# Global attention scores: q's low part against k's high part alone, in two 64-row halves of TensorE

## The chip, the cores and the metric

The kernel runs on one NeuronCore of a Trainium2 chip. The metric is the device time of one execution in microseconds (us). The profile comes from one execution on the chip, recorded by the hardware profiler; its times count from the first instruction.

## What is computed

One layer of a diffusion backbone over 1024 latent tokens of width 1024, with 256 context tokens. The input is modulated by a conditioning vector and projected. Two attention branches work on the projections: a windowed one (branch 0, the key blocks next to a block of 128 queries, a sink logit for each head) and a global one (branch 1, all keys, with root-mean-square norm of q and k). Both add the context's keys to the same softmax. Each branch has 8 query heads of width 64 and 2 key heads. Their outputs are gated, merged and projected; a feed-forward part with a short convolution follows. Cut to what the change touches:

```python
def _gqa_scores(q, k):
    return jnp.einsum("bqhgd,bkhd->bhgqk", q, k).astype(jnp.float32) * (HEAD_DIM ** -0.5)

def _global_attention(q, k_all, v_all):
    ...
        p = jax.nn.softmax(_gqa_scores(q_blk, k_all), axis=-1)
        return _gqa_values(p, v_all)
```

## The kernel before

Most products are formed from split numbers: a float32 value is stored as a high part, rounded to the format that TensorE reads in one pass (R32), and a low part, the rest (`split`, line 80). `mm3` (line 89) then needs three matmuls: high by high, high by low, low by high.

The projections come first. The windowed q, the k and v of both branches and the gates are computed group by group; PSUM tiles are emptied by a queue of small steps (`side_step`, line 681). `kv_post` (line 343) handles one tile of 128 tokens of k and v: step `s1` stores v and starts norm and rotary, `s2` ends them and splits the four key heads (two of each branch) into `ks` (line 370), a tile of 128 tokens by 4 heads by 128 columns: 64 columns of k's high part, then 64 of its low part. `s3` transposes each head on TensorE (line 376), so that the high part comes to lie in partitions 0 to 63 and the low part in 64 to 127, and ScalarE copies the result into `KL[h]` (line 379; 128 partitions by 1024 tokens). Context keys go to `KC` (line 381).

Attention is cut into 32 units (`class Unit`): 16 of the windowed branch, then 16 of the global one. A unit is one block of 128 queries and one key head, with its 4 query heads. `qprep` (line 397) runs two units ahead: GpSimd splits q into `qs`, high part and low part next to each other; four transposes (line 404) bring it into a PSUM tile `tr` (high in partitions 0 to 63, low in 64 to 127; inside attention this tile comes from the pool `pt` of three, which the transposes of the probabilities use too). ScalarE copies it into `q1` (line 407), and two DMAs of SP's queue (lines 408 and 409) write the halves of `q1` into the other halves of `q2`. So `q1` holds high over low, and `q2` low over high.

`qk` (line 412) makes one score tile with two matmuls over all 128 rows: `q1` against k gives high by high plus low by low, `q2` against k gives low by high plus high by low. The sum is the product with all four terms. `lat` (line 425) does a head: in the global branch it calls `qk` for each half of 512 of the 1024 latent keys (lines 441 and 442), each half into its own PSUM bank of the tile `s`. VectorE then scales and takes the maximum (line 459), ScalarE exponentiates (line 426). `cxp` (line 464) does the context's keys for the four heads of a global unit. `value_steps` transposes the probabilities (`ptr`, line 531), splits them (`pth`, `ptl`, lines 540 and 541, some on GpSimd) and multiplies with v (`av`, lines 552 and 553); `rows` (line 496) transposes the sums of the softmax (`str`, line 498).

The steps of a unit's scores, of the values of the unit before and, from the third global unit on, of the windowed branch's output product (`branch_steps`, tiles `b`, lines 90 to 92 by `mm3`) are interleaved in the main loop (line 833). A scheduler of the language's tile layer orders the instructions of each engine from there, within the dependencies, before the program is built; each engine then runs its own list in order.

Of the kernel before, what the change touches and what calls it, by code (L numbers as in the profile page):

```python
# [7 lines left out]
F32 = mybir.dt.float32  # L8
# [5 lines left out]
P = 128  # L14
D = 1024
T = 1024
NC = 256
KT = 8
NT = 8
HD = 64  # L20
# [7 lines left out]
HALF = 512  # L28
# [41 lines left out]
def layer_kernel(  # L70
# [6 lines left out]
    nc = tc.nc  # L77
# [152 lines left out]
    for k in range(KT):  # L230
# [5 lines left out]
        for t in range(NT):  # L236
            s = slice(t * P, (t + 1) * P)
# [96 lines left out]
    KL, KC, VT = [], [], []  # L334
# [8 lines left out]
    def kv_post(t, kv):  # L343
        st = {}
        kb = kv[:, 128:256].rearrange("p (h d) -> p h d", d=HD)

        def s1():
            vt = VT[t // 2][:, t % 2]
            v3 = kv[:, 256:512].rearrange("p (h d) -> p h d", d=HD)
            nc.scalar.copy(vt[:, :, 0:HD], v3)  # L350
            tp = pw(f"ktp{t}")
            st["tp"] = tp = [tp[:, n * P:(n + 1) * P] for n in range(4)]
            st["ss"] = rms_scale(kb, 2, f"k{t}", tp[3])
            if t < NT:
                st["tb"] = ph1.tile([P, 2, HD], F32, tag="tb", name=f"tbk{t}", bufs=4)
                gfold(st["tb"], 1, t, nc.vector)
                rope(nc.vector, kv[:, 0:128], kv[:, 0:128], 2, ropec[:, t], ropes[:, t], f"ka{t}", tp[0], tp[1])
            nc.gpsimd.tensor_tensor(out=vt[:, :, HD:P], in0=v3, in1=vt[:, :, 0:HD].bitcast(F32), op=ALU.subtract)

        def s2():  # L360
            rms_apply(kb, 2, st["ss"])
            tp = st["tp"]
            if t < NT:
                tb = st["tb"]
                rope(nc.vector, kv[:, 128:256], kv[:, 128:256], 2, tb[:, 0], tb[:, 1], f"kb{t}", tp[2], tp[3])
            else:
                nc.gpsimd.tensor_tensor(out=kb, in0=kb, in1=bc(gcol[:, 1], 2), op=ALU.mult)
            st["ks"] = ks = pw(f"ks{t}", (P, 4, P), R32)
            k3 = kv[:, 0:256].rearrange("p (h d) -> p h d", d=HD)
            split(k3, ks[:, :, 0:HD], ks[:, :, HD:P], nc.vector, nc.vector)  # L370

        def s3():
            ks = st["ks"]
            tr = acc_tile(f"ktr{t}", R32).rearrange("p (h q) -> p h q", h=4)
            for h in range(4):
                nc.tensor.transpose(tr[:, h], ks[:, h], identr)
            if t < NT:
                for h in range(4):
                    nc.scalar.copy(KL[h][:, t * P:(t + 1) * P], tr[:, h])
            else:  # L380
                nc.scalar.copy(KC[0][:, :, (t - NT) * P:(t - NT + 1) * P], tr)
        return [s1] + [lambda: None] * GAP + [s2, s3]

    class Unit:
# [12 lines left out]
        def qprep(self, mk=None):  # L397
            nm = self.id
            q3 = qtile(self.br, self.i)[:, self.g * 256:(self.g + 1) * 256].rearrange("p (h d) -> p h d", d=HD)
            qs = qp.tile([P, 4, P], R32, tag="qs", name=f"qs{nm}", bufs=1)  # L400
            split(q3, qs[:, :, 0:HD], qs[:, :, HD:P], nc.gpsimd, nc.gpsimd)
            tr = (mk or pt_tile)(f"qtr{nm}", R32)
            for h in range(4):
                nc.tensor.transpose(tr[:, h * P:(h + 1) * P], qs[:, h], identr)
            q1 = qp.tile([P, 512], R32, tag="q1", name=f"q1{nm}", bufs=2)
            q2 = qp.tile([P, 512], R32, tag="q2", name=f"q2{nm}", bufs=2)
            nc.scalar.copy(q1, tr)
            nc.sync.dma_start(q2[0:HD].bitcast(F32), q1[HD:P].bitcast(F32))
            nc.sync.dma_start(q2[HD:P].bitcast(F32), q1[0:HD].bitcast(F32))
            self.q = q1, q2  # L410

        def qk(self, o, h, ks, stop=True):
            hs = slice(h * P, (h + 1) * P)
            nc.tensor.matmul(o, self.q[0][:, hs], ks, start=True, stop=False)  # L414
            nc.tensor.matmul(o, self.q[1][:, hs], ks, start=False, stop=stop)  # L415

        def begin(self):
            self.nm = small(f"nm_{self.id}", (P, 4))
# [9 lines left out]
        def lat(self, h):  # L428
# [9 lines left out]
                self.qk(s[:, 256:512], h, KC[0][:, kh])  # L438
                o = s
            elif self.br == 1:  # L440
                for c in (0, 512):
                    self.qk(s[:, c:c + 512], h, KL[kh][:, c:c + 512])
                o = s
            else:
                w = self.w
                l = s[:, 512 - w:512]
                self.qk(l, h, KL[kh][:, self.k0:self.k0 + w], False)
                if w == 384:
                    nc.tensor.matmul(l.rearrange("p (a b) -> p a b", b=P)[:, 0::2, :], identr, maskr,
                                     start=False, stop=True)  # L450
                elif self.i == 0:
                    nc.tensor.matmul(l[:, 128:256], identr, maskr[:, 1], start=False, stop=True)
                else:
                    nc.tensor.matmul(l[:, 0:128], identr, maskr[:, 0], start=False, stop=True)
                self.qk(s[:, 512:512 + NC], h, KC[0][:, kh])
                o = s[:, 512 - w:512 + NC]
# [1280 lines left out]
```

## Time and profile before

| what | value |
|---|---|
| median of 3 runs | 1587.79 us (1587.26 to 1591.52) |
| span of the profiled execution | 1585.4 us |
| PE busy | 1528.4 us, 96% |
| DVE busy | 1195.6 us, 75% |
| ACT busy | 813.0 us, 51% |
| POOL busy | 753.7 us, 48% |
| mean granted TensorE clock | 0.992 of full speed |
| attention, first to last score matmul | 343.3 to 756.7 us |

The profiled execution's own time is its span; its distance to the median is 2.4 us. Engines: PE is TensorE's matmul side, PEld its weight loads, which overlap with matmuls; DVE is VectorE, ACT ScalarE, POOL GpSimd, SP SyncE, which issues most DMAs. A matmul's record ends later than the start of the next one, because matmuls are pipelined and their ends are modelled: the step from start to start is what a matmul takes of TensorE. A line of a group names source line, engine, operation, output and inputs, shapes and count, then busy us and mean ns of one, then the idle time before it and what ended it.

### The profile page before, as it was taken

What the parts mean: (1) busy time and instruction counts of PE and PEld (TensorE: products, weight loads), DVE (VectorE), ACT (ScalarE), POOL (GpSimd) and SP (SyncE); (2) the same over time, 40 slices, a digit from 0 to 9 for tenths busy, and PEclk for the clock granted to TensorE, in tenths of its full rate; (3) what the DMA queues carried; (4) which work ended last, traced back from release to release, by engine and by line L of the source; (5) the groups of instructions that cost most, each with busy time, mean ns of one, the idle gap of its engine ahead of it and who ended that gap; (6) DMA issues with size and microseconds to landing.
All of it is one profiled execution on the core that took longest, in us unless ns stands there. A gap on an engine that the chain in (4) does not pass through costs nothing.

```text
span 1585.4 us, 22064 instructions
## 1 busy us (share of the span) xinstructions
PE 1528.4 (96%) x7680; PEld 1269.8 (80%) x7680; DVE 1195.6 (75%) x1766; ACT 813.0 (51%) x1443; POOL 753.7 (48%) x731
## 2 busy tenths in 40 slices
PE   6999999999999999999999999999999999999996
PEld 5878788878887887777788898888888888888876
DVE  7797646628888777888674779888888877657886
ACT  5422222448887667688531565444444444435642
POOL 0574302426667556665422554666667764021132
PEclk9999999999999999999999999999999999999998
DMA  9695662322236555531451132333334446996721
GB/s 378 217 313 188 221 217 81 120 80 67 62 104 157 139 127 145 118 73 39 142 186 53 60 101 86 114 107 112 115 106 118 111 113 189 358 273 210 255 94 53
DMA packets 112367, 229.98 MB, mean 145 GB/s; under 512 B 12960, under 2 KB 27808, under 8 KB 112160
## 3 DMA queue, kind: packets, MB, share of 16 engines
q1 hardware_dynamic: 96816, 198.93, 37.6%
q0 software_dynamic: 10400, 20.19, 8.2%
q10 hardware_dynamic: 5040, 9.46, 1.6%
q8 instruction: 60, 0.98, 0.3%
q14 instruction: 51, 0.42, 0.1%
HBM read 177.35 MB, written 65.86 MB: 153 GB/s over the span
## 4 chain that ended last, share of the span: by engine, by line
PE 82%; DVE 6%; ACT 4%; issue 3%; POOL 2%; DMA 2%; ACTq 0%; SPq 0%; DVEq 0%; POOLq 0%
PE ptr L531 5%; PE p L90 4%; PE p L91 4%; PE p L92 4%; PE g L90 3%; PE g L91 3%; PE g L92 3%; PE b L92 3%; PE b L91 3%; PE b L90 3%; PE s L414 2%; PE a L92 2%; PE c L91 2%; PE d L91 2%; PE c L92 2%
## 5 line engine op out<-in xcount | busy, mean ns | idle before, releaser
L541 DVE TENSOR_TENSOR ptl<-ptr,pth 128x512 fp32r<-128x512 f32 x188 | 124.8, 685 | 27.5 <-ACT pth L540 25.2
L531 PE MATMUL ptr<-ident,p 128*128 128x128 f32 x816 | 126.5, 278 | 10.3 <-DVE ptl L541 7.8
L540 ACT CAST pth<-ptr 128x512 fp32r<-128x512 f32 x188 | 106.6, 588 | 56.3 <-PE ptr L531 32.7
L87 DVE TENSOR_TENSOR ld<-rd,hd 128x1024 fp32r<-128x1024 f32 x77 | 94.0, 1240 | 52.5 <-ACT hd L82 50.4
L426 ACT ACTIVATE p<-p,nm 128x1024 f32<-128x1024 f32 (+2 forms) x128 | 125.3, 981 | 10.9 <-DVE p L459 10.1
L531 PEld LDWEIGHTS ptr<-ident,p 128*128 128x128 f32 x816 | 93.8, 140 | 40.3 <-DVE ptl L541 13.5
L82 ACT CAST hd<-rd 128x1024 fp32r<-128x1024 f32 x77 | 79.2, 1050 | 81.5 <-PE p L92 50.0
L552 PE MATMUL av<-pth,VT 128*128 128x512 f32 x236 | 104.6, 443 | 1.0 <-ACT avs L558 0.5
L90 PE MATMUL p<-hd 128*128 128x512 f32 x264 | 103.2, 391 | 0.0
L92 PE MATMUL p<-hd,ld 128*128 128x512 f32 x264 | 102.7, 389 | 0.0
L91 PE MATMUL p<-ld,hd 128*128 128x512 f32 x264 | 102.7, 389 | 0.0
L90 PE MATMUL g<-hh,whg 128*128 128x512 f32 x256 | 99.9, 390 | 0.0
L92 PE MATMUL g<-hh,wlg 128*128 128x512 f32 x256 | 99.7, 389 | 0.0
L91 PE MATMUL g<-hl,whg 128*128 128x512 f32 x256 | 99.6, 389 | 0.0
L553 PE MATMUL av<-ptl,VT 128*128 128x512 f32 x236 | 97.6, 414 | 2.0 <-POOL ptl L87 1.9
L87 POOL TENSOR_TENSOR wlg<-wg,whg 128x512 fp32r<-128x512 f32 x32 | 47.0, 1479 | 109.6 <-ACT whg L82 107.3
L459 DVE TENSOR_SCALAR_CACHE_REDUCE p<-s,cvt,nmc 128x1024 f32<-128x1024 f32 x64 | 84.5, 1340 | 12.3 <-PE s L415 11.8
L414 PE MATMUL s<-KL,q 128*128 128x512 f32 (+2 forms) x192 | 76.0, 396 | 2.9 <-ACT p_x L426 2.0
L188 DVE CUSTOM_DVE_ANT_0 wml<-wml,sc,bmc 128x1024 f32<-128x1024 f32 x32 | 45.0, 1416 | 39.0 <-DMA wml<-in_wmodT_dram 38.6
L84 POOL TENSOR_SCALAR pth<-prw 128x512 fp32r<-128x512 f32 x48 | 31.1, 649 | 88.2 <-ACT prw L537 62.7
L82 ACT CAST wS<-s 128x512 fp32r<-128x512 f32 x76 | 45.3, 621 | 52.1 <-POOL s L1079 51.3
L415 PE MATMUL s<-KL,q 128*128 128x512 f32 (+2 forms) x192 | 71.7, 373 | 0.0
(396 smaller groups left out, 4974.0 us busy)
## 6 DMA issues: line engine op xcount, KB each, us to landing
wml<-in_wmodT_dram SPq DMA_DIRECT2D x48, 512.0 KB
ru<-in_w_up_dram SPq DMA_DIRECT2D x38, 512.0 KB
rd<-td SPq DMA_DIRECT2D x55, 256.0 KB
rd<-sd SPq DMA_DIRECT2D x44, 256.0 KB
rd<-in_w_dn_dram SPq DMA_DIRECT2D x33, 256.0 KB
wm<-in_wmodT_dram SPq DMA_DIRECT2D x16, 512.0 KB
wg<-in_w_g_dram SPq DMA_DIRECT2D x32, 256.0 KB
sgd<-sg ACTq DMA_DIRECT2D x32, 256.0 KB
```

Of the source, the lines that this page charges most:

```text
L82: nc.scalar.copy(hi, src)
L87: lo_eng.tensor_tensor(out=lo, in0=src, in1=hi.bitcast(F32), op=ALU.subtract)
L90: nc.tensor.matmul(ps, a[0], b[0], start=start, stop=False, skip_group_check=resumed)
L91: nc.tensor.matmul(ps, a[0], b[1], start=False, stop=False, skip_group_check=resumed)
L92: nc.tensor.matmul(ps, a[1], b[0], start=False, stop=stop, skip_group_check=resumed)
L414: nc.tensor.matmul(o, self.q[0][:, hs], ks, start=True, stop=False)
L426: nc.scalar.activation(p, s, AF.Exp, bias=nm[:, h:h + 1], scale=scale, accum_out=sm[:, h:h + 1])
L531: nc.tensor.transpose(tr[:, h * P:(h + 1) * P], self.pslice(h, n), ident)
L540: nc.scalar.copy(hi, tr)
L541: nc.vector.tensor_tensor(out=lo, in0=tr, in1=hi.bitcast(F32), op=ALU.subtract)
L552: nc.tensor.matmul(self.av, v, hi, start=first, stop=False)
L553: nc.tensor.matmul(self.av, v, lo, start=False, stop=self.left == 0)
```

## The change

In the global branch the high by low term is moved into the first matmul, and the low by low term is dropped. `q1` now holds the high part in both halves, `q2` the low part in both. The first matmul (`q1` against k, 128 rows) gives high by high plus high by low. The second needs k's high part alone, which is 64 rows. `qk_pair` issues both 512-column halves together: two matmuls of 128 rows, then one of 64 rows in the upper half of TensorE's rows and one of 64 rows in the lower half. For that, k's high part must lie in partitions 64 to 127 for the second half of the tokens: `kv_post` stores the two heads of the global branch (`hs` 2 to 4) with the halves swapped for token tiles 4 to 7, and does the split in two pieces there. The windowed branch and the context keys still use `qk` with all 128 rows: with the new `q1` and `q2` it sums the same four terms as before.

```diff
             k3 = kv[:, 0:256].rearrange("p (h d) -> p h d", d=HD)
-            split(k3, ks[:, :, 0:HD], ks[:, :, HD:P], nc.vector, nc.vector)
+            a, b = slice(0, HD), slice(HD, P)
+            for hs, hi, lo in (((slice(0, 2), a, b), (slice(2, 4), b, a)) if NT // 2 <= t < NT else
+                               ((slice(0, 4), a, b),)):
+                split(k3[:, hs], ks[:, hs, hi], ks[:, hs, lo], nc.vector, nc.vector)
...
-            nc.scalar.copy(q1, tr)
-            nc.sync.dma_start(q2[0:HD].bitcast(F32), q1[HD:P].bitcast(F32))
-            nc.sync.dma_start(q2[HD:P].bitcast(F32), q1[0:HD].bitcast(F32))
+            nc.scalar.copy(q1[0:HD], tr[0:HD])
+            nc.sync.dma_start(q1[HD:P].bitcast(F32), q1[0:HD].bitcast(F32))
+            nc.scalar.copy(q2[HD:P], tr[HD:P])
+            nc.sync.dma_start(q2[0:HD].bitcast(F32), q2[HD:P].bitcast(F32))
             self.q = q1, q2
...
+        def qk_pair(self, o, h, ks):
+            hs = slice(h * P, (h + 1) * P)
+            for n in (0, 1):
+                nc.tensor.matmul(o[n], self.q[0][:, hs], ks[n], start=True, stop=False)
+            for n, g in enumerate((slice(0, HD), slice(HD, P))):
+                nc.tensor.matmul(o[n], self.q[1][g, hs], ks[n][g], start=False, stop=True)
...
             elif self.br == 1:
-                for c in (0, 512):
-                    self.qk(s[:, c:c + 512], h, KL[kh][:, c:c + 512])
+                cs_ = slice(0, HALF), slice(HALF, T)
+                self.qk_pair([s[:, c] for c in cs_], h, [KL[kh][:, c] for c in cs_])
                 o = s
```

## The prediction, made before the changed kernel ran

> **What bounds the kernel now.** I began with the page's table of engines, its slices and the shares of the chain, to see which engine sets the pace.
>
> ```profile
> span 1585.4 us, 22064 instructions
> PE 1528.4 (96%) x7680; PEld 1269.8 (80%) x7680; DVE 1195.6 (75%) x1766; ACT 813.0 (51%) x1443; POOL 753.7 (48%) x731
> ...
> PE   6999999999999999999999999999999999999996
> ...
> PEclk9999999999999999999999999999999999999998
> ...
> PE 82%; DVE 6%; ACT 4%; issue 3%; POOL 2%; DMA 2%; ACTq 0%; SPq 0%; DVEq 0%; POOLq 0%
> ```
>
> TensorE is busy in every slice at full granted clock and carries 82% of the chain. But this is an average, and the change sits in attention alone. So I asked for the busy time of each engine by stretch: the end of the projections (260 to 343 us), the windowed branch (343 to 470), the first two units of the global branch (470 to 508), the global units with the windowed branch's output matmuls mixed in (508 to 654; these tiles b start at 508.1), and the global units without them (654 to 764).
>
> ```profile
> core 0: us, PE busy (x) PEld busy (x) DVE busy (x) ACT busy (x) POOL busy (x), PEclk, DMA share, GB/s
> 260.00:343.00 83.00, 82.98 (x392) 68.64 (x391) 41.82 (x139) 27.86 (x78) 26.33 (x30) 1.00 0.28 92
> 343.00:470.00 127.00, 121.69 (x820) 103.97 (x818) 107.62 (x254) 106.53 (x254) 79.28 (x112) 1.00 0.28 77
> 470.00:508.00 38.00, 34.24 (x197) 26.18 (x196) 32.58 (x61) 33.32 (x82) 25.82 (x38) 1.00 0.70 169
> 508.00:654.00 146.00, 143.89 (x806) 118.38 (x805) 107.17 (x186) 97.73 (x212) 83.58 (x112) 1.00 0.57 136
> 654.00:764.00 110.00, 102.20 (x599) 81.37 (x597) 95.46 (x162) 87.70 (x195) 66.93 (x96) 1.00 0.28 60
> ```
>
> From 508 to 654 us TensorE stands idle for only 146 - 143.89 = 2.1 us, and no other engine is over 74% busy: TensorE time saved there is time saved. In 470 to 508 and 654 to 764 it idles for 3.8 and 7.8 us while VectorE is 86 to 87% and ScalarE 80 to 88% busy: part of a saving there will turn into waits. In the windowed branch ScalarE is already 106.53 / 127 = 84% busy and TensorE 96%.
>
> The price of one matmul is the step between starts, not its recorded length. One stretch of TensorE's timeline shows it (columns: start, length in us, engine, line, operation).
>
> ```profile
> 605.49 1.03 PE L531 MATMUL ptr<-ident,p 128*128 128x128 f32 x8
> 606.28 0.49 PE L552 MATMUL av<-pth,VT 128*128 128x512 f32 x1
> 606.61 0.40 PE L553 MATMUL av<-ptl,VT 128*128 128x512 f32 x1
> 606.85 0.40 PE L552 MATMUL av<-pth,VT 128*128 128x512 f32 x1
> 607.08 0.40 PE L553 MATMUL av<-ptl,VT 128*128 128x512 f32 x1
> ...
> 607.77 0.40 PE L414 MATMUL s<-KL,q 128*128 128x512 f32 x1
> 608.00 0.39 PE L415 MATMUL s<-KL,q 128*128 128x512 f32 x1
> 608.23 0.40 PE L414 MATMUL s<-KL,q 128*128 128x512 f32 x1
> 608.47 0.40 PE L415 MATMUL s<-KL,q 128*128 128x512 f32 x1
> 608.70 0.27 PE L498 MATMUL str<-ident,sm 128*4 128x128 f32 x1
> 608.73 0.48 PE L90 MATMUL b<-O,hwb 128*128 128x512 f32 x1
> 609.04 0.39 PE L91 MATMUL b<-O,hwb 128*128 128x512 f32 x1
> ```
>
> A score matmul of 512 columns takes 0.23 us of TensorE (607.77 to 608.70: 0.93 for four); the record, 0.39, runs some 0.16 past the next start. Eight transposes take 0.79 us, 0.10 each, and the first 512-column matmul after them holds TensorE 0.33 instead of 0.23: a turn from transposes back costs 0.10.
>
> **The change, part by part.** (1) *Scores of the global branch*: 16 units of 4 heads. Each head keeps two matmuls of 128 rows and has its other two replaced by two of 64 rows, in different row groups and different PSUM tiles. Side by side the pair costs 0.23, one after the other 0.46. No 64-row matmul is in this trace. The nearest row for an added cost is the 0.10 after a transpose, a weight load that nothing hid: if the second half's load starts only behind the first half's matmul, the pair costs 0.33. I take 0.28, the middle of 0.23 and 0.33, since half of that load may hide: a gain of 0.18 per head.
>
> In the instruction order of the changed kernel, 52 of the 64 pairs are adjacent; the scheduler has put transposes, and in places value or output matmuls, inside the other 12. Those cannot run together and gain nothing. I charge a split pair 0.05 for its extra turns (0 to 0.10, the turn above): 12 x 0.05 = 0.6 us lost. Of the 52, 30 lie in the units with mixed-in work and 22 in the others. In the first everything counts: 30 x 0.18 = 5.4 us. In the others the trace shows waits on VectorE and ScalarE that stay; I count half: 22 x 0.18 / 2 = 2.0 us.
>
> The page "TensorEngine Tiling (Array Packing)" of the Trainium skill, section "Key Properties", says that tiles run independently but that a change of tiling mode drains TensorE. The trace has one change of mode, the transpose str with a 4-column stationary: from 608.47 to 609.04 stand two 512-column matmuls and this transpose, 0.57 - 2 x 0.23 = 0.11 for the transpose and both turns, where a transpose alone is 0.10. So this row shows hardly any drain; whether row groups behave like it, no row here shows, and it is a rival below.
>
> (2) *q's preparation*, in all 32 units: one copy out of PSUM becomes two of 64 partitions.
>
> ```profile
> L407 ACT CAST q<-qtr x32: 560/577/617, 286.6 to 730.2; 128x512 fp32r<-128x512 f32 x32
> L408 SPq DMA_DIRECT2D q<-q x32: 461/500/1684, 287.3 to 730.8; - x32
> L409 SPq DMA_DIRECT2D q<-q x32: 577/588/603, 287.9 to 731.3; - x32
> ```
>
> The groups of the windowed stretch alone, 343 to 470 us (busy us, mean ns, then idle before and what ended it):
>
> ```profile
> L531 PE MATMUL ptr<-ident,p 128*128 128x128 f32 x284 | 48.3, 281 | 1.9 <-DVE ptl L541 0.7 <-ACT p L426 0.7 <-ACT rb L501 0.2
> ...
> L407 ACT CAST q<-qtr 128x512 fp32r<-128x512 f32 x15 | 8.6, 576 | 0.1
> ...
> L501 ACT COPY rb<-str 4x128 f32<-4x128 f32 x14 | 3.6, 254 | 5.6 <-issue 2.1 <-PE str L498 2.0 <-POOL ot L566 1.0
> ```
>
> A 64x512 copy stands in no row: the ends are 0.25 us (4x128) and 0.58 (128x512). I take 0.58, since 512 columns remain. ScalarE gains 0.58 per unit: 15 x 0.58 = 8.7 us in the windowed stretch, to 115 of 127 us, 91%; in the three global stretches it stays below 93%. The PSUM tile is released one copy later, and the softmax exponentials and transposed casts behind the copy on ScalarE start later, on which VectorE and then TensorE's next transpose wait. The two DMAs stay two. The second is issued 0.58 later and holds SP's queue that long, ahead of the rb rows and bT loads; q1 now waits for a landing too, where only q2 did, and L415 followed L414 by 0.23, so that wait is new by 0.23 at most. Both are needed only two units later: cost 0, and if that cover were gone 0.58 + 0.23 for a unit.
>
> ```profile
> PEld ptr L531 <- ACT q L407: 3.8, 12, 0.3
> ```
>
> This row of the waits (us in total, times, longest) in the same stretch is the weak spot: weight loads already wait twelve times for q's copy, hidden so far behind running matmuls. On the other side stands the new order. Turns from transposes to other matmuls in the windowed branch fall from 90 to 67, and in the global branch rise from 122 to 127, counting those into 64-row halves. 23 x 0.10 = 2.3 us gained, 5 x 0.10 = 0.5 lost, the latter inside the charge for split pairs. For the windowed branch the ends are -2.3 us (new order, copies hidden) and 8.7 - 2.3 = +6.4 (copies wholly exposed). I take 0, towards the lower end: some 2.3 us of the copies come through, no more, because TensorE's transposes themselves, in the row above (x284), show no idle time that q's copy ended.
>
> (3) *k's split*: for four key tiles VectorE does four smaller instructions instead of two.
>
> ```profile
> L86 DVE CAST ks<-kv x10: 280/291/1364, 261.2 to 315.3; 128x256 fp32r<-128x256 f32 x10
> L87 DVE TENSOR_TENSOR ks<-kv,ks x10: 409/420/1391, 261.5 to 316.7; 128x256 fp32r<-128x256 f32 x10
> ```
>
> At most they double: 4 x (0.29 + 0.42) = 2.8 us, at least 0. In 260 to 343 us TensorE is busy for 82.98 of 83 us and VectorE for 41.82, so they are hidden; I take 0, and 2.8 if that cover failed.
>
> **Sum**: -5.4 - 2.0 + 0.6 + 0 + 0 = -6.8 us. The work after attention keeps its order. The profiled execution has a span of 1585.4; the median of the runs is 1587.79, 2.4 above it, which I carry over: span 1578.6, time **1581.0 us**.
>
> **The rivals.**
> *Pairs wholly side by side* (0.23 each, and TensorE sets the pace in all global units): 52 x 0.23 = 12.0 us less 0.6, so 1576.4; with the 2.3 of the new order 1574.1. For it: TensorE's 82% of the chain. Against it: VectorE and ScalarE at 80 to 88% from 654 us. The page "TensorE: Matmul & The Clock Gate" of the Trainium skill, section "Measured speedup vs the span model", gives about 4 ns per further tile, which is this rival; no run here shows it yet.
> *ScalarE takes over in the windowed branch*: its copies are wholly exposed, +6.4, against -6.8: 1587.4. For it: the twelve waits. Against it: 16% of ScalarE still free.
> *The halves run one after the other*: the change doesn't do what it says. No gain, +0.6: 1588.4.
> *A drain at each change of row group* (slower): if TensorE empties before and after each pair, each turn costs the 0.16 us by which the record outlasts the step. An adjacent pair then loses 0.32 - 0.23 = 0.09, in all 52 x 0.09 = 4.7; a split pair has four turns and no gain, 12 x 0.64 = 7.7: +12.4, 1600.2. It decides from 0.115 per turn, where two eat up the 0.23. For it: the rule above. Against it: the str row.
>
> **How the numbers follow.** Forecast 0.43, wholly side by side 0.20, ScalarE 0.15, one after the other 0.12, drain 0.10. The range runs from 1574, the best rival with the new order, to 1591, which takes in the serial case with 2.6 us of k's split or q's copies; only the drain and the tails lie outside. A measurement of this kernel can tell about 0.3% (4.8 us) from no change, so faster means under 1583.0. Faster: 0.78 of the forecast (its 6.8 is close to the bound) and the first rival, 0.54. Within: the rest of the forecast and most of the ScalarE and serial cases, 0.31. Slower: the drain and the tails of those two, 0.15.
>
> **What would show it.** In TensorE's timeline the two 64-row matmuls of an adjacent pair should start less than 0.1 us apart and the next matmul about 0.28 us after the first; 0.46 means serial, and above that, drains. The stretch of units with b tiles should shorten from 146 to about 141 us, the global units without them by some 2 us together, and the windowed branch should stay near 127 us with ScalarE at 91%. I am wrong if transposes there begin to wait for the second q copy, or if the units from 654 us shorten by nothing because VectorE sets their pace.

## The result and the profile after

The changed kernel takes 1604.11 us (median of 4 runs, 1603.88 to 1605.90), the kernel before 1588.94 (4 runs, 1587.26 to 1591.52). The ratio is 1.0096 with an interval of 1.0082 to 1.011: 15 us slower. The ratios, here and below, go over all the runs and differ a little from the quotient of the two medians. Forecast were 1581.0 us and a range of 1574 to 1591, so time and sign were both wrong.

The page's first lines and the chain's shares, of the kernel after:

```profile
span 1602.4 us, 22145 instructions
...
PE 1540.9 (96%) x7680; PEld 1254.4 (78%) x7680; DVE 1202.6 (75%) x1774; ACT 833.1 (52%) x1475; POOL 758.5 (47%) x731
...
PE 76%; DVE 9%; POOL 4%; DMA 4%; ACT 3%; issue 3%; ACTq 0%; SPq 0%; DVEq 0%; POOLq 0%
```

The span grew by 17.0 us. TensorE has as many matmuls as before (7680) but is busy for 12.5 us longer, and its share of the chain fell from 82 to 76%: two things happened, TensorE work got dearer, and other engines came onto the path. To see where, I split attention by three marks: the first score matmul, the first context score of the global branch (`s_x`) and the last score. They stand in the rows of the tiles `s` and `s_x` (columns: duration min/median/max in ns, first to last start in us, shapes). Before:

```profile
L414 PE MATMUL s<-KL,q x192: 278/394/504, 343.3 to 756.5; 128*128 128x512 f32 x128, 128*128 128x384 f32 x48, 128*128 128x256 f32 x16
L415 PE MATMUL s<-KL,q x192: 278/389/487, 343.5 to 756.7; 128*128 128x512 f32 x128, 128*128 128x384 f32 x48, 128*128 128x256 f32 x16
...
L414 PE MATMUL s_x<-KC,q x64: 278/282/390, 470.8 to 747.2; 128*128 128x256 f32 x64
```

After:

```profile
L426 PE MATMUL s<-KL,q x128: 491/498/502, 484.7 to 774.4; 64*128 64x512 f32 x128
L418 PE MATMUL s<-KL,q x64: 277/339/443, 345.1 to 478.8; 128*128 128x384 f32 x48, 128*128 128x256 f32 x16
...
L418 PE MATMUL s_x<-KC,q x64: 278/282/387, 482.7 to 764.7; 128*128 128x256 f32 x64
```

| stretch | before | after | difference |
|---|---|---|---|
| start to first score | 343.3 | 345.1 | +1.8 |
| A: windowed branch, first score to first `s_x` | 127.5 | 137.6 | +10.1 |
| B: global branch, first `s_x` to last score | 285.9 | 291.7 | +5.8 |
| last score to the end | 828.7 | 828.0 | -0.7 |

The 1.8 us of the start are spread between executions: the experiments below have their first score anywhere from 342.5 to 346.5 us. The change costs 10 us in the windowed branch, whose scores it does not touch, and 6 us in the global branch, where a gain of 7.4 less 0.6 was forecast. The busy times of the two stretches say that these are different losses. Before:

```profile
core 0: us, PE busy (x) PEld busy (x) DVE busy (x) ACT busy (x) POOL busy (x), PEclk, DMA share, GB/s
343.30:470.80 127.50, 122.06 (x823) 104.14 (x821) 108.42 (x256) 107.27 (x257) 79.35 (x113) 1.00 0.28 78
470.80:756.70 285.90, 272.61 (x1551) 220.20 (x1552) 227.65 (x391) 211.95 (x473) 170.85 (x235) 1.00 0.49 114
```

After:

```profile
core 0: us, PE busy (x) PEld busy (x) DVE busy (x) ACT busy (x) POOL busy (x), PEclk, DMA share, GB/s
345.10:482.70 137.60, 125.50 (x827) 106.14 (x825) 111.87 (x257) 117.96 (x273) 81.70 (x114) 1.00 0.27 72
482.70:774.40 291.70, 283.60 (x1551) 205.74 (x1548) 225.83 (x391) 220.59 (x487) 169.06 (x235) 1.00 0.49 112
```

In B the same 1551 matmuls are busy for 283.60 instead of 272.61 us, 11.0 more; 5.2 of that came out of TensorE's idle time, which fell from 13.3 to 8.1. That is a price of the matmuls themselves. It shows in the time only where TensorE had little idle time: the first ten global units, with the windowed branch's output matmuls in most of them, took 200.0 us instead of 193.7, the last six 91.6 instead of 92.3, although TensorE was busy for 4.4 us more in these too. In A TensorE's idle time rose from 5.4 to 12.1 us: that is waiting, 6.7 of the 10.1. The other 3.4 are busy time, in part of the four more matmuls that fall into the stretch; they were not followed further. By the first score matmul of the last windowed unit 6.9 of the 10.1 us have gathered; the other 3.2 come in the one step from there to the first `s_x`. ScalarE stands at 117.96 of 137.60, 86%, not at the 91% forecast, since the stretch grew with it.

**What a pair costs.** TensorE's timeline of the kernel after, a stretch of the global branch (neighbours of one line are put together: x2 are two matmuls):

```profile
611.29 0.39 PE L564 MATMUL av<-ptl,VT 128*128 128x512 f32 x1
611.52 0.63 PE L424 MATMUL s<-KL,q 128*128 128x512 f32 x2
612.08 0.49 PE L426 MATMUL s<-KL,q 64*128 64x512 f32 x2
612.50 0.73 PE L424 MATMUL s<-KL,q 128*128 128x512 f32 x2
613.16 0.49 PE L426 MATMUL s<-KL,q 64*128 64x512 f32 x2
613.59 0.55 PE L542 MATMUL ptr<-ident,p 128*128 128x128 f32 x3
```

The two halves together have a record of 0.49 us, as one half alone has (498 ns in the row of L426): they do run side by side. The single records give starts 3 ns apart (median of 52 pairs). But the two 128-row matmuls ahead of the pair take 0.56 (611.52 to 612.08) instead of 0.46, and the pair takes 0.42 (612.08 to 612.50) instead of 0.23. The next two, right behind a pair, take 0.66, since the first of them, too, takes 0.34. The median steps from start to start agree: 231 ns from one 128-row score matmul to the next, 326 from a 128-row to a 64-row matmul, 427 from a 64-row to whatever comes next. So the turn in costs 0.095 and the turn out 0.196 us: 0.29 for a pair that saves 0.23. The waits of the weight loads show the same turn, 484 to 765 us (us in total, times, longest):

```profile
PEld s L426 <- issue: 22.8, 71, 0.4
```

71 weight loads of 64 rows stand for 0.32 us each with nothing that the profile names to wait for. Between two 128-row score matmuls the step stays at 231 ns, so the weight load there is hidden; this one is not.

**What holds the windowed branch.** The timeline of ScalarE and TensorE around q's copies, one unit of the kernel before:

```profile
402.17 0.46 PE L404 MATMUL qtr<-identr,qs 128*128 128x128 f32 x4
...
404.56 0.58 ACT L407 CAST q<-qtr 128x512 fp32r<-128x512 f32 x1
...
405.19 0.55 PE L531 MATMUL ptr<-ident,p 128*128 128x128 f32 x3
```

and of the kernel after:

```profile
417.50 0.47 PE L407 MATMUL qtr<-identr,qs 128*128 128x128 f32 x4
...
419.87 0.56 ACT L410 CAST q<-qtr 64x512 fp32r<-64x512 f32 x1
...
420.71 0.20 ACT L503 ACTIVATE f<-f 128x4 f32<-128x4 f32 x1 [0.28 <-DVE f L502]
...
420.94 0.58 ACT L412 CAST q<-qtr 64x512 fp32r<-64x512 f32 x1
...
421.57 0.55 PE L542 MATMUL ptr<-ident,p 128*128 128x128 f32 x3 [0.37 <-ACT q L412]
```

Before, the PSUM tile of q's transposes is taken at 402.17 and free at 405.14, 2.97 us; after, from 417.50 to 421.52, 4.02 us: the second copy adds 0.58, and another 0.51 pass between the two. Three such tiles serve all transposes, and the next one, `ptr`, wants it at once: TensorE idles 0.37 us for the second copy. The medians over the windowed units (first transpose to the end of the last copy) are 2.96 and 4.02 us. The waits from 343 to 483 us add it up, before:

```profile
PE ptr L531 <- ACT q L407: 0.6, 1, 0.6
```

and after:

```profile
PE ptr L542 <- ACT q L412: 3.0, 8, 0.5
```

This is the sign that the prediction had named for being wrong: transposes wait for the second copy, eight times instead of once. Yet 3.0 us are not 10. The experiments had to say whether the copies, their landings, the new layout or the new order of instructions make up the rest.

### The profile page after: what moved, and what is told of

Same layout as the page of the kernel before. It is cut to its first block, busy times and chain, and to the rows that moved or that the text cites. A ratio compares the mean times of both kernels' runs of the same rounds, so it can differ in the third digit from the quotient of the medians.

```text
span 1602.4 us, 22145 instructions
## 1 busy us (share of the span) xinstructions
PE 1540.9 (96%) x7680; PEld 1254.4 (78%) x7680; DVE 1202.6 (75%) x1774; ACT 833.1 (52%) x1475; POOL 758.5 (47%) x731
## 4 chain that ended last, share of the span: by engine, by line
PE 76%; DVE 9%; POOL 4%; DMA 4%; ACT 3%; issue 3%; ACTq 0%; SPq 0%; DVEq 0%; POOLq 0%
PE ptr L542 5%; PE p L90 4%; PE p L92 4%; PE p L91 4%; PE b L92 3%; PE b L90 3%; PE b L91 3%; PE a L90 2%; PE d L90 2%; PE c L90 2%; PE c L91 2%; PE d L91 2%; PE a L91 2%; PE c L92 2%; PE a L92 2%
## 5 line engine op out<-in xcount | busy, mean ns | idle before, releaser
L542 PEld LDWEIGHTS ptr<-ident,p 128*128 128x128 f32 x816 | 90.4, 140 | 40.9 <-DVE ptl L552 10.4
L470 DVE TENSOR_SCALAR_CACHE_REDUCE p<-s,cvt,nmc 128x1024 f32<-128x1024 f32 x64 | 84.2, 1338 | 12.1 <-PE s L426 11.5
L82 ACT CAST wA<-ru 128x512 fp32r<-128x512 f32 x57 | 35.5, 623 | 61.5 <-PE d L92 33.3
L87 POOL TENSOR_TENSOR ptl<-prw,pth 128x512 fp32r<-128x512 f32 x48 | 63.6, 1326 | 3.1
```

The lines of the kernel that those rows point to most:

```text
L82: nc.scalar.copy(hi, src)
L87: lo_eng.tensor_tensor(out=lo, in0=src, in1=hi.bitcast(F32), op=ALU.subtract)
L470: nc.vector.tensor_scalar(out=p, in0=o, scalar1=self.qscale(nqs)[:, hs] if self.br else -1.0, scalar2=self.other[:, hs], op0=ALU.mult, op1 ...
L542: nc.tensor.transpose(tr[:, h * P:(h + 1) * P], self.pslice(h, n), ident)
```

## The experiments

Theory one (turns): in the global branch each stretch of 64-row matmuls pays a turn in and a turn out that together cost more than the pair saves. Its rivals: the pairs gain as forecast, and the loss there comes from q's preparation; or the halves are not side by side. Theory two (hold): the windowed branch loses because two copies hold the PSUM tile longer. Its rivals: ScalarE's added 0.58 us per unit; the later landings or the third wait; and the order that the scheduler made of it.

In the tables A and B are the stretches defined above, in the profiled execution; "unit" is the spacing of the windowed units in their steady part (before 8.39 us, after 8.89).

### The parts alone: e1, e2, e3

**e1**: the changed kernel without the pairs, q's new preparation alone.

```diff
-                cs_ = slice(0, HALF), slice(HALF, T)
-                self.qk_pair([s[:, c] for c in cs_], h, [KL[kh][:, c] for c in cs_])
+                for c in (0, 512):
+                    self.qk(s[:, c:c + 512], h, KL[kh][:, c:c + 512])
```

With q's new layout and k's swapped halves, `qk` over all 128 rows still sums all four terms.

> The changed kernel, but the global branch's scores keep two matmuls of 128 rows for each column block: q's preparation (two copies out of PSUM, two DMAs) and k's swapped halves stay, no 64-row matmul is left. It sums all four terms, as the kernel before. Theory A (q's second copy on ScalarE, and the order that the scheduler builds around it, cost the windowed branch its 10 us): the windowed branch, from its first score matmul to the first of the global branch's context scores, takes 136 to 138 us against 127.5 before, the global branch as long as before (286 us), in all 1597 to 1602. Theory B (the 64-row matmuls cost nearly everything, and the windowed branch lost its time because the scheduler ordered it around them): the windowed branch at 127 to 129 us, the time within 0.2% of before, 1586 to 1591.

**e2**: the kernel before with k's swapped halves alone (the change's first hunk).

> The kernel before, with k's swapped halves alone (four smaller VectorE instructions in place of two for four key tiles; the two full matmuls of a score tile sum the same four terms whichever way the halves lie). Theory A and Theory B both: nothing, 1587 to 1591, since TensorE covers it. A rival, that the split delays the end of the projections (the changed kernel's first score matmul started 1.8 us later): 1589.5 to 1592, with the first score matmul at about 345 us in its profile.

**e3**: the change with the old single copy of q. The windowed branch keeps its two DMAs and its layout; the global units make the new layout with three. k's split and the pairs are those of the change.

```diff
             nc.scalar.copy(q1, tr)
             nc.sync.dma_start(q2[0:HD].bitcast(F32), q1[HD:P].bitcast(F32))
-            nc.sync.dma_start(q2[HD:P].bitcast(F32), q1[0:HD].bitcast(F32))
+            if self.br == 0:
+                nc.sync.dma_start(q2[HD:P].bitcast(F32), q1[0:HD].bitcast(F32))
+            else:
+                nc.sync.dma_start(q2[HD:P].bitcast(F32), q1[HD:P].bitcast(F32))
+                nc.sync.dma_start(q1[HD:P].bitcast(F32), q1[0:HD].bitcast(F32))
```

> The changed kernel's pairs, but with one copy of q out of PSUM as before: the windowed branch's units get the kernel before's two DMAs, the global units three DMAs that make high over high and low over low. Same result as the changed kernel. 56 of the 64 pairs are adjacent in its order. Theory A: the windowed branch back at 127 to 129 us, the global branch 4 to 6 us longer than before (each stretch of 64-row matmuls costs TensorE 0.09 us going in and 0.19 going out, 72 stretches x 0.29 = 21 us, less 56 x 0.23 = 13 that run side by side, in part hidden in waits), in all 1591 to 1595. Theory B: the windowed branch still near 137 us, 1600 to 1605.

| kernel | us (before beside it) | ratio, 95% | A | B | unit |
|---|---|---|---|---|---|
| e1 | 1600.83 (1589.20) | 1.0078, 1.0066 to 1.0090 | 138.4 | 287.2 | 8.89 |
| e2 | 1588.48 (1589.20) | 1.0000, 0.9991 to 1.0009 | 127.3 | 285.1 | 8.38 |
| e3 | 1596.87 (1589.20) | 1.0059, 1.0046 to 1.0072 | 129.7 | 291.4 | 8.39 |

k's split costs nothing. q's preparation alone brings the whole loss of A with hardly any of B; the pairs alone bring the whole loss of B with hardly any of A. The two losses are largely separate (alone they make 11.6 and 7.7 us, 19.3 in sum, where the change makes 15.2), and the pairs lose even where nothing of the preparation in the windowed branch is changed. e3 came out 1.9 us above the 1591 to 1595 expected. The 2.2 us that it loses in A lie wholly behind the last windowed unit's preparation, where the third DMA of the first global units stands; until there its units start within 0.1 us of those before. 1.4 of them are one wait of TensorE for a landing of q's DMAs, just ahead of the first `s_x`. e9 below shows the like; the kernel after, with two DMAs, has no such wait in attention.

### The turns: e6, e5, e11

**e6**: e3 with each half put right behind its own 128-row matmul, so that there are 128 stretches of 64-row matmuls instead of 72 and no pairs.

```diff
-            for n in (0, 1):
-                nc.tensor.matmul(o[n], self.q[0][:, hs], ks[n], start=True, stop=False)
             for n, g in enumerate((slice(0, HD), slice(HD, P))):
+                nc.tensor.matmul(o[n], self.q[0][:, hs], ks[n], start=True, stop=False)
                 nc.tensor.matmul(o[n], self.q[1][g, hs], ks[n][g], start=False, stop=True)
```

> As the run with pairs and the old preparation, but each 64-row half stands right behind its own 128-row matmul, so that no two halves can run together and there are 128 stretches of 64-row matmuls instead of 72. Same result. Theory of the turns (going into and out of a stretch costs 0.29 us together, halves side by side save 0.23): 56 x 0.29 + 56 x 0.23 = 29 us of TensorE more than with the pairs, of which four fifths or more show: 1614 to 1624. Rival, that 64-row matmuls are slow in themselves (0.42 us each, wherever they stand) and the turns cost nothing: 64-row matmuls that were side by side come one after the other, 56 x 0.42 = 24 us, 1612 to 1618, with no 128-row matmul delayed behind them in the timeline. Rival, that neither counts and the loss is waits on other engines: within 5 us of the run with pairs.

It took 1627.48 us beside 1589.20, ratio 1.0268 (1.0241 to 1.0296): 30.6 us above e3 for 56 more stretches, 0.55 each, where 0.29 and 0.23 were expected: the time lies above the 1614 to 1624 that the theory gave. A stays at 130.6. TensorE's timeline of e6:

```profile
612.32 0.39 PE L427 MATMUL s<-KL,q 128*128 128x512 f32 x1
612.63 0.49 PE L428 MATMUL s<-KL,q 64*128 64x512 f32 x1
613.06 0.50 PE L427 MATMUL s<-KL,q 128*128 128x512 f32 x1
613.49 0.50 PE L428 MATMUL s<-KL,q 64*128 64x512 f32 x1
613.92 0.27 PE L511 MATMUL str<-ident,sm 128*4 128x128 f32 x1
```

Between 128 and 64 rows each step is 0.43 us (612.63, 613.06, 613.49, 613.92): a head takes 1.60 instead of 0.92 before. The 128-row matmul between two stretches takes 0.43 as well, so it is not that 64-row matmuls are slow in themselves. The price goes with the number of turns, in doses. The profiled execution had a mean granted clock of 0.984 (at 612 us it was 1.00); the reading rests on the four executions at 0.990 to 0.993, which took 1625.78 to 1627.85 us.

**e5**: e3 with both halves in the upper row group (k not swapped).

```diff
-            for n, g in enumerate((slice(0, HD), slice(HD, P))):
+            for n, g in enumerate((slice(0, HD), slice(0, HD))):
```

> As the run with pairs and the old preparation, but both 64-row halves of a head lie in the upper row group (k is not swapped), at the same places of the order: 72 stretches as there, and no two halves in different row groups. Same result. If different row groups are what lets halves run together: the second half starts 0.23 us after the first instead of 0.004, 56 x 0.23 = 13 us of TensorE, 10 to 13 more than the 1596.9 there: 1606 to 1611. Rival, that the pair's 0.42 us is one 64-row matmul after the other in any case: the same time within 0.2%, 1594 to 1600.

It took 1605.61 us beside 1586.90, ratio 1.0110 (1.0091 to 1.0129), at the lower edge of the 1606 to 1611 expected, with B at 300.6. TensorE's timeline of e5:

```profile
606.79 0.63 PE L424 MATMUL s<-KL,q 128*128 128x512 f32 x2
607.35 0.73 PE L426 MATMUL s<-KL,q 64*128 64x512 f32 x2
608.01 0.73 PE L424 MATMUL s<-KL,q 128*128 128x512 f32 x2
608.68 0.73 PE L426 MATMUL s<-KL,q 64*128 64x512 f32 x2
609.34 0.55 PE L542 MATMUL ptr<-ident,p 128*128 128x128 f32 x3
```

In one row group the two halves take 0.66 us (607.35 to 608.01), in two row groups 0.42. The median step from half to half is 337 ns against 3. So different row groups are what puts the halves side by side, and this rival, that they are not, is out; B differs from that of e3 by 9.2 us, most of 56 x 0.24 = 13.4. The row groups do what the change says; the turns eat it.

**e11**: if turns are the price, two pairs for one turn should gain. e3 with the scores of two heads issued as four 128-row matmuls and then four of 64 rows.

```diff
+            self.wide(o[h], h, ks, True)
+            last = self.wide(o[h + 1], h + 1, ks, True)
+            for n in (h, h + 1):
+                for i in self.pair(o[n], n, ks, False):
+                    tc.add_manual_dep(i, last.name, NOSYNC, reason="two heads")
+            self.lat(h)
+            self.lat(h + 1)
```

> As the run with pairs and the old preparation, but the scores of two heads are issued together: four matmuls of 128 rows, then the four of 64 rows, held together in the order (27 of 32 groups have all four in a row, 37 stretches of 64-row matmuls instead of 72). Same result. Theory of the turns: 37 x 0.29 = 10.7 us against 59 halves side by side, 59 x 0.23 = 13.6, so TensorE has 3 us less to do than before; VectorE gets a head's scores later, which the units without other work may feel: 1584 to 1591, in any case 5 us or more under the 1596.9. Rival, that the loss of the global branch is in waits of VectorE and ScalarE and not in turns: no better than 1596, rather worse, since two score tiles are filled at once.

It took 1603.03 us beside 1586.90, ratio 1.0095 (1.0077 to 1.0112): the gain did not come. The theory's 1584 to 1591 was missed, and the time lies where the rival had put it. TensorE did get cheaper. Of the 32 groups 27 stayed whole, 37 stretches in all, and one group in e11's timeline reads:

```profile
604.31 0.73 PE L428 MATMUL s<-KL,q 128*128 128x512 f32 x2
604.97 0.73 PE L433 MATMUL s<-KL,q 64*128 64x512 f32 x4
605.63 0.55 PE L564 MATMUL ptr<-ident,p 128*128 128x128 f32 x3
```

Two pairs take 0.66 us together, where in e3 each takes 0.43. From 484 to 765 us TensorE is busy for 264.5 us, 7.3 less than in e3. But it is idle for that much more, 16.5 us instead of 9.2. Waits in that stretch, of e3:

```profile
DVE p L473 <- PE s L429: 12.0, 15, 1.5
POOL p_x L501 <- ACT f L498: 9.6, 12, 1.8
```

Of e11:

```profile
POOL p_x L518 <- ACT f L515: 18.0, 9, 5.7
DVE p L476 <- PE s L433: 16.9, 12, 2.2
...
PE s_x L422 <- DMA q<-q: 4.8, 1, 4.8
```

VectorE's scaling waits 16.9 us for scores instead of 12.0, now that a head's scores end only with those of the next one, and GpSimd waits 18.0 instead of 9.6 for what the softmax makes of them. These waits cost time only where TensorE comes to wait in turn: its own waits for the softmax's results (`p_x`, `p`, `sm`) rose from 3.0 to 6.2 us. The largest new wait of TensorE is another, a single one of 4.8 us for a landing of q's DMAs, ahead of the second global unit's context scores. Right behind it, from 492.6 to 500 us, the granted clock was 0.50 to 0.66, and 1.00 again at 500; that is most of the reason why the profiled execution was granted 0.97 from 484 to 654 us, where e3 had 1.00. Its one execution at a mean of 0.994 took 1599.69 us, still 12.8 above the kernel before beside it, where e3 was 7.7 above; whether that one had the long wait is not on record. So the steps show the cheaper turns and the time does not, and since a late landing and a lower clock stand beside them, e11's time does not test the theory. Why the landing was late, and whether the number of score tiles sets the softmax's part, was not tried.

### The windowed branch: e7, e8, e9, e10

Each of these is the kernel before with one part of q's new preparation. **e7**, the copy in two pieces of 64 partitions, everything else old:

```diff
-            nc.scalar.copy(q1, tr)
+            nc.scalar.copy(q1[0:HD], tr[0:HD])
+            nc.scalar.copy(q1[HD:P], tr[HD:P])
```

> The kernel before with one edit: q is copied out of PSUM in two pieces of 64 partitions into the old layout, the DMAs as before. ScalarE has as much more to do as in the changed kernel, and q1 and q2 wait for no other landings than before. Theory A1 (the second copy, by ScalarE's time and by holding the PSUM tile): the windowed branch at 135 to 139 us, 1595 to 1600. Theory A2 (the changed layout: the first matmul waits for a landing, the second DMA is issued later): the windowed branch at 127 to 129 us, 1587 to 1591.

**e8**, the copy in two pieces of 256 columns, each over all partitions:

```diff
-            nc.scalar.copy(q1, tr)
+            nc.scalar.copy(q1[:, 0:256], tr[:, 0:256])
+            nc.scalar.copy(q1[:, 256:512], tr[:, 256:512])
```

> The kernel before with q copied out of PSUM in two pieces of 256 columns (all 128 partitions) instead of one of 512: a smaller dose of the same thing, two copies that together take some 0.7 to 0.8 us in place of 0.58 (0.58 is mostly columns), against 1.15 with two pieces of 64 partitions. If the loss of the windowed branch goes with the time of the copies: a quarter to a third of its 10 us, 129 to 131 us, 1589 to 1592. Rival, that a second instruction on the tile is what counts, whatever it takes: 136 us and more, 1597 and more.

**e9**, one copy, the new layout by three DMAs in all units:

```diff
-            nc.sync.dma_start(q2[HD:P].bitcast(F32), q1[0:HD].bitcast(F32))
+            nc.sync.dma_start(q2[HD:P].bitcast(F32), q1[HD:P].bitcast(F32))
+            nc.sync.dma_start(q1[HD:P].bitcast(F32), q1[0:HD].bitcast(F32))
```

> The kernel before with q laid out as in the changed kernel (high over high, low over low), made by one copy and three DMAs in all 32 units; scores by two full matmuls, the same four terms. q1 now waits for a landing, and later than in the changed kernel, since its DMA follows two others. Theory A1 (the copy): the windowed branch at 127 to 130 us, 1587 to 1592. Theory A2 (landings): as long as in the changed kernel or longer, 137 us and more, 1597 and more.

**e10**, one copy and a second one of 64x512 that reads SBUF, not PSUM; its output is overwritten:

```diff
             nc.scalar.copy(q1, tr)
+            nc.scalar.copy(q2[0:HD], q1[0:HD])
```

> The kernel before with one more ScalarE copy of 64x512 per unit, right behind q's copy but from SBUF to SBUF (into the half of q2 that the first DMA then overwrites): ScalarE is as busy as with two copies, but the PSUM tile is released after the first. If ScalarE's time makes the loss: the windowed branch at 135 to 139 us, 1595 to 1601, as with two copies. If holding the PSUM tile makes it: 127 to 130 us, 1587 to 1591.

"Hold" is the median time from q's first transpose to the end of the last copy out of its PSUM tile, over the windowed units of the trace.

| kernel | us (before beside it) | ratio, 95% | A | B | unit | hold |
|---|---|---|---|---|---|---|
| before | | | 127.5 | 285.9 | 8.39 | 2.96 |
| after | 1604.11 (1588.94) | 1.0096, 1.0082 to 1.011 | 137.6 | 291.7 | 8.89 | 4.02 |
| e7, two by partitions | 1600.73 (1586.90) | 1.0085, 1.0068 to 1.0103 | 137.6 | 287.4 | 8.88 | 4.02 |
| e8, two by columns | 1590.07 (1588.94) | 1.0011, 0.9997 to 1.0025 | 128.9 | 284.2 | 8.41 | 3.02 |
| e9, three DMAs | 1593.10 (1586.90) | 1.0030, 1.0016 to 1.0044 | 130.6 | 286.5 | 8.25 | 2.94 |
| e10, copy from SBUF | 1588.64 (1588.94) | 1.0003, 0.9991 to 1.0015 | 127.9 | 285.1 | 8.26 | 2.96 |

The loss goes with the partition split: e7 alone makes it whole, in A to the tenth of a us. It is not ScalarE's time (e10 adds as much, 0.62 us per unit), not the number of copies (e8 has two) and not the layout (e9's units are not longer; its 3 us lie at the branch's two ends, where TensorE waits 1.3 and 1.4 us for landings of q's DMAs, and its time is 1 us above the 1587 to 1592 expected). The kernels whose hold stays near 3 us keep units of 8.25 to 8.41 us; the ones with 4.02 have 8.9. But these also share a new order of TensorE's list, with 75 turns from transposes to other matmuls in A by the traces, where the others have 104 to 106; so these runs alone do not part the hold from the order. What sets e8's split apart stands in the copies' rows. Of e8:

```profile
L407 ACT CAST q<-qtr x32: 346/363/452, 287.8 to 732.0; 128x256 fp32r<-128x256 f32 x32
L408 ACT CAST q<-qtr x32: 352/378/463, 288.1 to 733.5; 128x256 fp32r<-128x256 f32 x32
```

Half the columns cost 0.36 to 0.38 us, half the partitions 0.56 to 0.58 in the timeline of the kernel after, as much as the whole tile before (0.58).

### Hold or order: e12, e13

With two copies by partitions the scheduler also makes another order of TensorE's list in the windowed branch (that of e1, e7 and the kernel after is one and the same there). So the list was forced: the matmuls and transposes of attention are recorded, and each is held behind its forerunner in a list written down in the kernel.

```diff
+        for x, y in zip(seq, seq[1:]):
+            tc.add_manual_dep(y, x.name, NOSYNC, reason="order")
```

**e12**: the kernel before, with its one copy, in the order of e7.

> The kernel before (one copy of q) with TensorE's attention instructions held to the order that the scheduler built for two copies in the old layout (in the windowed branch the changed kernel has that same order). Theory O (the new order makes the loss): the windowed branch at 134 to 139 us, 1594 to 1601. Theory H (holding q's PSUM tile until the second copy makes it, whatever the order): 127 to 130 us, 1587 to 1591.

**e13**: e7, with its two copies, in the order of the kernel before.

> The other way round: two copies of q in the old layout, with TensorE's attention instructions held to the order of the kernel before. Theory O: the windowed branch at 127 to 130 us, 1587 to 1592. Theory H: 135 us and more, 1595 and more, with transposes waiting for the second copy.

| kernel | us (before beside it) | ratio, 95% | A | B | unit | hold |
|---|---|---|---|---|---|---|
| e12, new order, one copy | 1598.23 (1588.54) | 1.0059, 1.0036 to 1.0082 | 138.4 | 284.5 | 9.01 | 1.65 |
| e13, old order, two copies | 1613.82 (1588.54) | 1.0162, 1.0141 to 1.0182 | 136.9 | 302.8 | 8.88 | 3.56 |

Either alone gives about the whole loss of A, 10.9 and 9.4 us beside 10.1: e12 came out as theory O had it, e13 as theory H had it. The old order forced onto one copy was not run; e12's B, 284.5 beside 285.9 before, speaks against a price of the forcing itself. In the old order the hold is paid in waits. The first copy of e13 ends 2.96 us after q's first transpose, as before; the second adds 0.60 to the hold, and the units are 0.49 longer. From 343 to 483 us:

```profile
PE ptr L148 <- ACT q L469: 8.4, 13, 0.9
```

TensorE waits 8.4 us for the second copy, thirteen times, of the 9.4 that A is longer; in B, where the scheduler knew a better order as well, e13 loses another 16.9. In the new order the loss sits elsewhere, though the tile is free after 1.65 us. The waits of e12, 343 to 483 us:

```profile
DVE ot L628 <- POOL up L625: 13.3, 12, 1.6
POOL ot L631 <- DVE ot L628: 12.4, 13, 1.5
...
PE av L149 <- ACT avs L623: 5.0, 10, 0.9
...
PE av L149 <- POOL ptl L139: 3.6, 7, 1.4
```

Here the value matmuls wait 5.0 us for their accumulator to be emptied and 3.6 for GpSimd's low parts, 8.6 together; TensorE had no such waits before except 1.4 and 0.3 us. So in the old order the second copy's hold makes the loss, and in the new one the order makes as much of it without any longer hold. Both begin with the copy split by partitions, since that is all that e7 changes. That the scheduler reorders to get round the longer hold is argued, not shown; its order costs as much in A as the hold would and saves 15 us in B (287.4 against 302.8). It also fits that the kernel after shows only 3.0 us of waits for the second copy.

## Why the prediction was wrong, point by point

**Scores of the global branch, -7.4 us: wrong, and this step failed by its size first.** "I take 0.28, the middle of 0.23 and 0.33": a pair takes 0.42 and its forerunner 0.10 more, together 0.52. The bound of 0.33 had been taken from a weight load behind transposes, a row of another kind; the turn itself was in no row. The sum with the measured steps: 52 adjacent pairs lose 52 x (0.52 - 0.46) = 3.1, where 0.46 is what the two matmuls of 128 rows cost before; 22 times a 128-row matmul stands right behind and takes 0.11 more, 2.4; a split pair pays both turns twice, 2 x (0.10 + 0.42) - 0.46 = 0.58, for 12 of them 7.0. That makes 12.5, beside 11.0 that TensorE is busier in B. Of these, 5.8 came through to the stretch; the rest went into idle time, in the last six units wholly. So "I count half", too, was a sound thought about a number of the wrong sign.

**The row that misled.** The str transpose with its 4-column stationary was read as "hardly any drain". It changes the columns in use, not the rows, and its turns stay next to nothing (0.11 with the transpose itself). Whether it is a change of tiling mode at all, no run shows; for a change of rows this row could not speak. "TensorEngine Tiling (Array Packing)" of the Trainium skill, section "Key Properties", says that a change of mode drains TensorE. The trace agrees as far as the price goes, 0.095 in and 0.196 out; whether a drain makes it, or the weight load that stands in the open, no run parts. "TensorE: Matmul & The Clock Gate" of the Trainium skill, section "Measured speedup vs the span model", gives about 4 ns for each further tile. Inside a pair the trace agrees, with 3 ns.

**Split pairs, +0.6: wrong by the same turn**, 0.58 each by the sum above instead of 0.05.

**q's preparation in the windowed branch, 0: wrong, the larger part, +10.1.** "I take 0 [...] because TensorE's transposes themselves [...] show no idle time that q's copy ended." The place was named, with its twelve waits as the weak spot, and a 64x512 copy did cost the 0.58 taken. What failed was to read hidden waits as cover that would stay. In the old order they came into the open: TensorE waits 8.4 us for e13's second copy, and 0.60 us more of hold costs 0.49 a unit. The changed kernel pays by its new order instead, 10.9 us in e12 even with one copy. The price was bounded by ScalarE's added time (8.7 us at most), which costs nothing in e10, and so the upper end of +6.4 was too low.

**The turns counted in the order, -2.3: wrong.** Fewer turns from transposes to matmuls were read as a cheaper order. e12 runs that order by itself, and A is 10.9 us longer. The order's price lies in what waits for what, not in its turns.

**k's split, 0: right** (e2: 1.0000, 0.9991 to 1.0009). q1's new wait for a landing, 0: right for the windowed branch, since e7 has no such wait and its A is the same 137.6.

**The rivals.** The drain at each change of row group, with a chance of 0.10, was the right one for B. Its turn of 0.16 put 0.09 on an adjacent pair (measured 0.06, or 0.17 with a 128-row matmul behind it) and 0.64 on a split one (0.58), and its 0.115 per turn as the point of decision stands: the two turns measured 0.29 together, 0.145 each. It gave 1600.2, within 4 us of the result, but partly by chance, since it had nothing for A, 10.1 us, and no idle time that took up its price, 12.4 where B grew by 5.8. "ScalarE takes over" had the right place and the wrong mechanism. Wholly side by side was true of the halves and untrue of the time.

**The signs.** Starts under 0.1 us apart: seen, 3 ns. The next matmul 0.28 after the first: 0.42. The stretch with b tiles shorter by 5 us: its first and last b tile stood 153.6 us apart before (the last at 661.7 us, not at 654) and 157.2 after. The global units without them shorter by 2 us: the last six took 92.3 and 91.6. There TensorE's idle time, 6.9 us before, was filled by the turns. The windowed branch near 127 us: 137.6. ScalarE at 91%: 86%.

**Open.** Why the new order's unit takes 8.9 to 9.0 us whatever the hold is shown only by its waits, not by a cause that was taken away; and why the scheduler chose it was not looked into. Where the 3.4 us more of TensorE's busy time in A come from is open. In e11 the low clock stands right behind a wait of 4.8 us. In e6 the granted clock was 0.50 from 500 to 508 and from 746 to 754 us with no wait of TensorE over 0.8 us in the 20 and the 10 us ahead; why was not tried.

## What to carry to other kernels

A stretch of matmuls on part of the rows had a price on both sides here, more than one pair saved; two pairs in one stretch were cheaper in the steps, though no run gained time by it. So count stretches, not matmuls, and look for the row of that very turn before pricing it. A wait that shows on weight loads but not on matmuls was here a resource with little slack left: price anything that holds it longer at nearly its full length. And if a scheduler orders the list, a small edit at one place can reorder a whole stage: read the profile by stages before looking at the code that was edited.

## What the runs showed of the hardware beyond that

- A 64-row stretch costs 0.095 us in and, behind one pair, 0.196 out, for matmuls of 512 columns at full clock, and a 128-row matmul right behind takes another 0.11; two pairs in a row take 0.66 with the turn out (e11), and two halves in one row group 0.66 (e5): there the second half starts 0.11 us later than a 128-row matmul would (337 against 231 ns).
- A copy out of PSUM on ScalarE over half the partitions takes as long as one over all of them (medians of 0.57 and 0.58 us for 64x512, 0.58 for 128x512); over half the columns it takes 0.36 to 0.38.
- 0.62 us more of ScalarE per unit cost nothing and left it 88% busy in A (e10), while 0.60 us more of a PSUM tile's hold cost 0.49 us per unit in one and the same order of TensorE's list (e13).
- Behind a single wait of TensorE of 4.8 us the granted clock was 0.50 to 0.66 for some 7 us (e11).
